# Seven block products in the down projection, weight sums made in DRAM, value columns copied by ScalarE

## The chip, the cores and the metric

The kernel runs on one core of a Trainium2 chip. The metric is the device time of one execution in microseconds, the median of the runs shown. Times within an execution come from the hardware profiler and are counted from the first instruction.

## What is computed

One layer of a hybrid encoder block on 512 tokens of width 1024, after 16 learned meta tokens:

```python
xn = rmsnorm(h, norm_mix_g)
sb_q, sb_k, sb_v, df_q, df_k, df_v = split(xn @ w_in)       # 8 heads of 128 in each of the two branches
o_sb = stick_breaking_attention(sb_q, sb_k, sb_v)           # strictly causal per frame, no softmax
o_df = rmsnorm(differential_attention(df_q, df_k, df_v))    # two softmax maps, block-causal chunks of 64
gates = sigmoid(xn @ w_gate + b_gate)
merged = gates[0] * (o_sb @ w_br_sb) + gates[1] * (o_df @ w_br_df)
h = h + merged @ w_out
hn = rmsnorm(h, norm_ffn_g)
a = silu(hn @ w_ffn_gate) * (hn @ w_ffn_up)                 # 512 x 2816
h = h + a @ w_ffn_down                                      # 2816 x 1024: the down projection
y = rmsnorm(h, norm_final_g)                                # the 512 tokens, meta tokens dropped
```

All data is float32. To keep its precision, the kernel cuts each operand of a product into a high part (a copy rounded to the matmul format) and a low part (what the rounding left), and makes three matmuls for each block: high by high, high by low, low by high. This is `split` (L74 to L76) and `mm3` (L224 to L229). The copy is a ScalarE cast, the difference a VectorE subtraction.

## The kernel before

**Weights.** `stream` lists all weights in the order of their use, in chunks of 512 KB: `cols` are 1024 rows by 128 columns, `rows` are 256 rows by 512 columns. `stage_one` (L128 to L145) issues the load of the next chunk from the SP queue into one of three buffers `wst` (`wsu` for some chunks). `generic` then splits it into `wh` and `wl`, of which there are four each. `READY` and `STAGE` say how many chunks ahead this is done.

**Heads.** The eight heads of the stick-breaking branch and then the eight of the differential branch are generators (`sb_head`, `df_head`). At each `yield n` the main loop (L927 to L962) runs n units of other work: projections for the next head (`halves`, `kv_units`, `seven_units`), parts of the branch output projection (`y_units`) and `turn`, which transposes the next head's values. From the third stick-breaking head on, its keys and values come from seven block products (`seven_units`).

`turn` (L464 to L478) transposes the value rows and gathers 16 columns from each 128 of them into `v_s`, by four GpSimd copies, which a fifth transposition then reads:

```python
for t in range(NQ):
    nc.gpsimd.tensor_copy(v_s[:, 32 * t:32 * t + NM], vT[:, (t + 1) * P:(t + 1) * P + NM])
nc.tensor.transpose(p5[:, 0:P], v_s, ident)
```

Other work of GpSimd in the heads: the bias of a differential head, its squares (`sq`, `sql`) for the head's norm, the stores of `y_units` to DRAM (from the third on they accumulate, L733), and transfers that swap the halves of the keys' high and low parts (`dk`, `dqk`, L620).

**SwiGLU.** For each 128 columns of the 2816, gate and up are made together by seven products of half-size blocks (`first`, `second`, `third`, with the weight sums of `c1` to `c4`). The result, transposed, is `aT`: 128 partitions by 22 row blocks by 512 tokens.

**Down projection.** `accumulate` (L1009 to L1048) runs over the two halves of 512 output columns; for each it goes through the 22 row blocks, and for each of these through four tiles of 128 tokens, with three matmuls of 512 columns a tile, into four banks. In the second half the last token tile is cut in two pieces of 256 columns, and the last six row blocks are done tile by tile, so that the tiles end one after the other. A finished bank is added to the residual `hres` by VectorE; then come the sum of squares (ScalarE), the gain (GpSimd), the root, the scaling and the store (`finish`). Weights for it are split by `generic`, activations by `act_parts`, each row block once for each half.

**Order.** The prologue is ordered by hand (`manual_schedule`); from `order.close()` (L923) on, a planner orders each engine's instructions by its own costs and by the order of the program. `tc.high_priority` moves single instructions ahead. Each engine works through its instructions in order.

Of the kernel before, what the change touches and what calls it, by code (L numbers as in the profile page):

```python
# [16 lines left out]
P = 128  # L17
# [23 lines left out]
def block_kernel(ctx: ExitStack, tc: tile.TileContext, x, meta, norm_mix_g, w_in, w_gate, b_gate,  # L41
# [31 lines left out]

    def split(hi, lo, src, lo_eng=None, hi_copy=None):  # L74
        (hi_copy or nc.scalar.copy)(hi, src)  # L75
        (lo_eng or nc.vector).tensor_tensor(lo, src, hi.bitcast(F32), op=ALU.subtract)  # L76
# [43 lines left out]
    first_ffn = at_of["fg", 1]  # L120
    staged, loaded = [], {}
# [6 lines left out]
    def stage_one():  # L128
        n = len(staged)
        if n == len(stream):  # L130
            return False
        key, view, c0, cw, k0, k1 = stream[n]

        if key[0] == "fu" and key[1]:
            if "w" not in fpools:
                return False
            st = fpools["w"].tile([P, KT, P], F32, tag="wsu", bufs=2, name="wsu")
        elif sevens(key) and key[2] == 1:
            st = fpools["a"].tile([P, KT, P], F32, tag="wsu", name="wsu")
        else:  # L140
            st = wpool.tile([P, k1 - k0, cw], F32, tag="wst", bufs=3, name="wst")
# [317 lines left out]
    def v_units(key, d):  # L459
        vT = d["vT"] = ap_.tile([P, L], F32, tag="vT", bufs=1, name="vT")  # L460

        def turn():
# [11 lines left out]
            for t in range(NQ):  # L474
                nc.gpsimd.tensor_copy(v_s[:, 32 * t:32 * t + NM], vT[:, (t + 1) * P:(t + 1) * P + NM])  # L475
# [450 lines left out]
    todo = []  # L926
    for br in range(2):  # L927
# [4 lines left out]
        for h in range(NH):  # L932
# [76 lines left out]
    def accumulate(pool, name, act, nk, half, tail, done, banks, pieces=None):  # L1009
# [6 lines left out]
        extra = z_tile()[:, 0] if pieces else None  # L1016

        def step(k, t, c0, c1):
# [3 lines left out]
            mm3((acc[t] if c0 == 0 else extra)[:, c0:c1],  # L1022
                [(ah[:, q], al[:, q], wh[:, k % 2, c0:c1], wl[:, k % 2, c0:c1])], k == 0, k == nk - 1)


        def cuts(t):
            return ((0, 256), (256, 512)) if t == NQ - 1 and pieces else ((0, 512),)

        for k in range(nk - tail):
            for t in range(NQ):  # L1030
                for c0, c1 in cuts(t):
                    step(k, t, c0, c1)
        for t in range(NQ):
            for c0, c1 in cuts(t):
                for k in range(nk - tail, nk):
                    step(k, t, c0, c1)
                cs = slice(half * 512 + c0, half * 512 + c1)
                nc.vector.tensor_tensor(hres[:, t, cs], hres[:, t, cs], (acc[t] if c0 == 0 else extra)[:, c0:c1], op=ALU.add)  # L1038
                sq = pool.tile([P, 512], F32, tag="y_sb", bufs=2, name="sq")
                s0, s1 = ssq[t][:, 0:1], ssq[t][:, 1:2]  # L1040
                nc.scalar.activation(sq[:, c0:c1], hres[:, t, cs], AF.Square, accum_out=(s1 if half else s0))
                if half == 0:
                    nc.vector.tensor_scalar(s0, s0, 1.0 / D, EPS, op0=ALU.mult, op1=ALU.add)
                elif c1 < 512:
                    nc.vector.scalar_tensor_tensor(s0, s1, 1.0 / D, s0, op0=ALU.mult, op1=ALU.add)
                if pieces:
                    pieces(t, cs)
# [90 lines left out]
    with tc.tile_pool(name="ffn", bufs=1) as fp:  # L1138
# [10 lines left out]
        jobs += [(generic, n) for n in range(at_of["down", 0, 0], len(stream))]  # L1149
# [61 lines left out]
        dw, acts = None, []  # L1211

        def act_parts(upto):

            for i in range(len(acts), min(2 * NFF, upto)):
                pool, tag, bufs = ((dw, "da", 4), (fw, ("wsu", "s21")[i % 2], 2))[i % 8 < 4]
                a = pool.tile([P, 2, SEQ], F32R, tag=tag, bufs=bufs, name="da")
                split(a[:, 0], a[:, 1], aT[:, i % NFF])
                acts.append(a)

        def act(half, k):
            act_parts(half * NFF + k + 3)
            return acts[half * NFF + k][:, 0], acts[half * NFF + k][:, 1]
# [22 lines left out]
        fpools["down"] = down_weights  # L1246
        ov = out[0].rearrange("(t p) d -> p t d", p=P)
# [50 lines left out]
```

## Time and profile before

| | us |
|---|---|
| median of 3 runs (lowest, highest) | 985.83 (984.46, 989.97) |
| the profiled execution, its span | 988.4, 986.6 |
| busy: TensorE, VectorE, ScalarE, GpSimd | 964.2, 670.7, 574.2, 170.1 |
| first and last matmul of the down projection | 854.82, 978.60 |

The span runs from the first to the last instruction; the execution's own time is 1.8 us longer. The profile names the tile that an instruction writes and those that it reads (`wl<-wst,wh`), its line (a helper's line stands for all that call it: L75 and L76 are the casts and subtractions of `split`, L227 to L229 the three matmuls of `mm3`), and, in brackets, how long the engine stood idle before it and what released it. PE is TensorE, DVE VectorE, ACT ScalarE, POOL GpSimd, SP the queue of plain transfers. Busy times of engines overlap; a wait costs something only where it lies on the way to the end.

### The profile page before, as it was taken

The numbers are of one execution on the slowest core, as the hardware profiler recorded it, in microseconds if no ns is written. First come the engines' busy times: TensorE is split into PE (matmuls) and PEld (weight loads), VectorE is DVE, ScalarE is ACT, GpSimd is POOL, SyncE is SP. The second block draws the span as 40 slices with busy tenths as digits, with TensorE's granted clock in tenths as the row PEclk, the third lists the DMA queues.
The fourth block names the chain that finished last, engine by engine and source line by source line (L and its number), as shares of the span: only waits on it lengthen the run. The fifth ranks groups of instructions, "written<-read, shape, count | busy, mean of one in ns | idle before, by whom it ended". The sixth has DMA issues, their size and how long they took to land.

```text
span 986.6 us, 16202 instructions
## 1 busy us (share of the span) xinstructions
PE 964.2 (98%) x6216; PEld 869.1 (88%) x6217; DVE 670.7 (68%) x1243; ACT 574.2 (58%) x1094; POOL 170.1 (17%) x214
## 2 busy tenths in 40 slices
PE   8899999999999999999999999989999999999996
PEld 6798888898899998899878888879999999988885
DVE  7798687766566876667724434798888888754644
ACT  7566666666566666666763433675555555743533
POOL 3300111111243322343225320000000000000103
PEclk9999999999999999999999999999999999999999
DMA  7312434455665533656659623232424333333212
GB/s 217 86 43 65 129 102 112 97 124 128 129 134 126 133 113 121 130 118 140 129 144 280 194 89 104 64 108 86 128 86 120 95 109 106 110 105 107 86 44 86
DMA packets 140240, 114.12 MB, mean 116 GB/s; under 512 B 4961, under 2 KB 115714, under 8 KB 140162
## 3 DMA queue, kind: packets, MB, share of 16 engines
q1 hardware_dynamic: 129810, 89.29, 30.0%
q0 software_dynamic: 10192, 23.73, 12.8%
q8 instruction: 49, 0.80, 0.3%
q14 instruction: 29, 0.24, 0.1%
q10 hardware_dynamic: 160, 0.07, 0.0%
HBM read 89.87 MB, written 18.87 MB: 110 GB/s over the span
## 4 chain that ended last, share of the span: by engine, by line
PE 90%; ACT 4%; DVE 4%; POOL 1%; issue 1%; DMA 0%; DVEq 0%; ACTq 0%; SPq 0%; POOLq 0%
PE mm L227 21%; PE mm L229 21%; PE mm L228 21%; PE z L227 6%; PE z L229 6%; PE z L228 6%; PE z L638 1%; PE z L637 1%; POOL v_s L475 1%; PE tr L493 1%; PE z L493 1%; PE tr L469 1%; ACT wh L75 1%; PE z L521 1%; DVE wl L76 0%
## 5 line engine op out<-in xcount | busy, mean ns | idle before, releaser
L76 DVE TENSOR_TENSOR wl<-wst,wh 128x1024 fp32r<-128x1024 f32 (+1 forms) x150 | 169.6, 1134 | 110.3 <-ACT wh L75 110.3
L75 ACT CAST wh<-wst 128x1024 fp32r<-128x1024 f32 (+1 forms) x150 | 146.2, 975 | 126.3 <-PE mm L228 70.0
L227 PE MATMUL mm<-xT_h,wh 128*128 128x264 f32 (+2 forms) x656 | 214.6, 327 | 0.5 <-ACT xT_h L830 0.5
L228 PE MATMUL mm<-xT_l,wh 128*128 128x264 f32 (+2 forms) x656 | 213.4, 325 | 0.5
L229 PE MATMUL mm<-xT_h,wl 128*128 128x264 f32 (+2 forms) x656 | 212.7, 324 | 0.0
L228 PEld LDWEIGHTS mm<-xT_l,wh 128*128 128x128 f32 x656 | 123.6, 188 | 10.3 <-DVE xT_l L831 1.3
L227 PEld LDWEIGHTS mm<-xT_h,wh 128*128 128x128 f32 x656 | 123.8, 189 | 10.0 <-ACT xT_h L830 0.9
L229 PEld LDWEIGHTS mm<-xT_h,wl 128*128 128x128 f32 x656 | 123.6, 188 | 10.0
L228 PE MATMUL mm<-hT_l,wh 128*128 128x256 f32 x284 | 80.5, 284 | 0.7 <-DVE hT_l L1081 0.7
L227 PE MATMUL mm<-hT_h,wh 128*128 128x256 f32 x284 | 80.1, 284 | 0.5 <-DVE sg L1176 0.5
L229 PE MATMUL mm<-hT_h,wl 128*128 128x256 f32 x284 | 80.1, 283 | 0.0
L475 POOL COPY v_s<-vT 128x16 f32<-128x16 f32 x64 | 31.9, 528 | 157.8 <-DVE vT L405 79.1
L228 PEld LDWEIGHTS mm<-hT_l,wh 128*128 128x128 f32 x284 | 53.7, 189 | 1.1 <-DVE hT_l L1081 1.1
L641 DVE CUSTOM_DVE_ANT_0 pr<-z,bias 128x144 f32<-128x144 f32 (+3 forms) x64 | 31.0, 502 | 34.9 <-PE z L638 34.7
L227 PEld LDWEIGHTS mm<-hT_h,wh 128*128 128x128 f32 x284 | 53.4, 189 | 0.9 <-DVE sg L1176 0.8
L229 PEld LDWEIGHTS mm<-hT_h,wl 128*128 128x128 f32 x284 | 53.6, 189 | 0.0
L227 PE MATMUL mm<-o_h,wh 128*128 128x512 f32 x128 | 53.1, 415 | 0.0
L229 PE MATMUL mm<-o_h,wl 128*128 128x512 f32 x128 | 50.8, 397 | 0.0
L228 PE MATMUL mm<-o_l,wh 128*128 128x512 f32 x128 | 50.1, 392 | 0.3 <-DVE o_l L709 0.3
L1262 POOL TENSOR_TENSOR outs<-hres,gF 128x512 f32<-128x512 f32 x4 | 5.1, 1291 | 262.3 <-DVE hres L1038 261.3
L227 PE MATMUL mm<-t_h,wh 128*128 128x256 f32 x168 | 47.5, 283 | 1.3 <-ACT wh L75 1.0
L228 PE MATMUL mm<-t_l,wh 128*128 128x256 f32 x168 | 47.3, 281 | 1.1 <-DVE t_l L1096 1.1
(330 smaller groups left out, 2534.3 us busy)
## 6 DMA issues: line engine op xcount, KB each, us to landing
wst<-in_w_in_dram SPq DMA_DIRECT2D x40, 512.0 KB, 4.2
wst<-in_w_ffn_gate_dram SPq DMA_DIRECT2D x22, 512.0 KB, 3.8
wst<-in_w_ffn_down_dram SPq DMA_DIRECT2D x22, 512.0 KB, 3.5
wsu<-in_w_ffn_up_dram SPq DMA_DIRECT2D x21, 512.0 KB, 3.8
y_df<-y_out POOLq DMA_DIRECT2D x32, 256.0 KB, 5.2
wst<-in_w_gate_dram SPq DMA_DIRECT2D x16, 512.0 KB, 5.5
wst<-in_w_br_sb_dram SPq DMA_DIRECT2D x8, 512.0 KB, 4.1
wst<-in_w_br_df_dram SPq DMA_DIRECT2D x8, 512.0 KB, 4.0
```

Of the source, the lines that this page charges most:

```text
L75: (hi_copy or nc.scalar.copy)(hi, src)
L76: (lo_eng or nc.vector).tensor_tensor(lo, src, hi.bitcast(F32), op=ALU.subtract)
L227: nc.tensor.matmul(ps, lhsT=ah, rhs=bh, start=(start and i == 0), stop=False, skip_group_check=skip)
L228: nc.tensor.matmul(ps, lhsT=ah, rhs=bl, start=False, stop=False, skip_group_check=skip)
L229: nc.tensor.matmul(ps, lhsT=al, rhs=bh, start=False, stop=(stop and i == n - 1), skip_group_check=skip)
L469: nc.tensor.transpose(pt[:, j * P:(j + 1) * P], vT[:, j * P:(j + 1) * P], ident)
L475: nc.gpsimd.tensor_copy(v_s[:, 32 * t:32 * t + NM], vT[:, (t + 1) * P:(t + 1) * P + NM])
L493: nc.tensor.transpose(pt[:, (t - j) * P:(t - j + 1) * P], blocks(t, j * P, (j + 1) * P), ident)
L521: nc.tensor.matmul(ps.rearrange("p (t q) -> p t q", q=P)[:, :, lo_rows:P], lhsT=vf[:, 1], rhs=a_s[:, 0:4 * qn], start=False, stop=True)
L637: nc.tensor.matmul(o, lhsT=q[c][:, qs], rhs=k[c][:, 0, k0:k1], start=True, stop=False)
L638: nc.tensor.matmul(o, lhsT=q[c][:, qs], rhs=k[c][:, 1, k0:k1], start=False, stop=True)
L641: nc.vector.tensor_tensor_reduce(po, zz, bb, scale=1.0, scalar=-3.0e38, op0=ALU.add, op1=ALU.max, accum_out=mx[:, t, c:c + 1])
```

## The change

The down projection is seen as a 2 x 2 product: the row blocks in two halves of 11, the output columns in two halves of 512, the tokens in two halves of 256. It is made by seven products of half-size blocks instead of eight, each 11 row blocks by 512 columns by 256 tokens. Three of the seven use raw blocks of the weights (a11, a12, a22), four use sums of blocks (s1 to s4); four use sums of blocks of the activations (t1 to t4), which VectorE makes during the stage.

The weight sums are made in DRAM during the heads, by 48 transfers on GpSimd's queue: 24 that copy a block, then 24 that accumulate onto it (`sum_job`). One is issued after every second unit of the heads, and each waits for the last ScalarE cast of `split` that stands before it in the program. The sums are then staged like other weights. In the stage, four more buffers for staged weights (`slots`) lie where the low parts of the SwiGLU's input were, and the block t2 where its high parts were.

In `turn`, one ScalarE copy of 64 columns takes the place of the four GpSimd copies.

```diff
     def split(hi, lo, src, lo_eng=None, hi_copy=None):
-        (hi_copy or nc.scalar.copy)(hi, src)
+        cast["last"] = (hi_copy or nc.scalar.copy)(hi, src)
...
-    for half in range(2):
-        for k0 in range(0, NFF, 2):
-            rows(("down", half, k0), w_fd, half * 512, k0)
+    NK = NFF // 2
+    DK = range(0, NK, 2)
+    w_sum = {(n, k0): sums_dram.tile([P, 2, 512], F32, name=f"d{n}_{k0}") for n in ("s1", "s2", "s3", "s4") for k0 in DK}
+    raw_at = {"a11": (0, 0), "a12": (NK, 0), "a21": (0, 512), "a22": (NK, 512)}
+    DOWN = (("a11", "b11", 0), ("a12", "b21", 1), ("s1", "t1", 2), ("s2", "t2", 0), ("s4", "b22", 2), ("s3", "t3", 0),
+            ("a22", "t4", 0))
...
+    def sum_job(to, of, k0, add):
+        src = raw_down(of, k0) if of in raw_at else w_sum[of, k0][:, 0:min(2, NK - k0)]
+        dst = w_sum[to, k0][:, 0:min(2, NK - k0)]
+        kw = dict(accum_op=ALU.add, max_dma_last_dim=2048) if add else {}
+        paced = mybir.DependencyInfo(mybir.DependencyClass.Sync, mybir.DependencyReason.DATA)
+        tc.add_manual_dep(nc.gpsimd.dma_start(dst, src, **kw).ins, cast["last"].ins.name, paced)
+
+    background = [(to, of, k0, i > 3) for i, (to, of) in enumerate(
+        (("s1", "a21"), ("s2", "a11"), ("s3", "a21"), ("s4", "a12"), ("s1", "a22"), ("s3", "a11"), ("s2", "s1"), ("s4", "s2")))
+        for k0 in DK]
...
+        if n >= first_down + 3 and "slots" not in fpools:
+            return False
...
+            slot = (n - first_down) % 7 - 3 if n >= first_down else -1
+            if slot < 0:
+                st = wpool.tile([P, 1024 // cw, cw], F32, tag="wst", bufs=3, name="wst")[:, 0:k1 - k0]
+            else:
+                st = fpools["slots"][:, slot, 0:k1 - k0]
...
-            for t in range(NQ):
-                nc.gpsimd.tensor_copy(v_s[:, 32 * t:32 * t + NM], vT[:, (t + 1) * P:(t + 1) * P + NM])
+            nc.scalar.copy(v_s.rearrange("p (t q) -> p t q", q=32)[:, :, 0:NM],
+                           vT[:, NM:L].rearrange("p (t q) -> p t q", q=P)[:, :, P - NM:P])
...
                 for _ in range(min(n, len(units))):
                     units.pop(0)()
+                    unit_count[0] += 1
+                    if background and unit_count[0] % 2 == 0:
+                        sum_job(*background.pop(0))
...
-                split(a[:, 0], a[:, 1], aT[:, i % NFF])
+                src, sign = block(b, k0), -1.0 if b == "t2" else 1.0
+                nc.scalar.activation(a[:, 0, 0:n], src, AF.Copy, scale=sign)
+                nc.vector.scalar_tensor_tensor(a[:, 1, 0:n], src, sign, a[:, 0, 0:n].bitcast(F32), op0=ALU.mult, op1=ALU.subtract)
...
+        def token_sum(name, k0):
+            b11, b12, b21, b22 = block("t1", k0), block("t3", k0), block("b21", k0), block("b22", k0)
+            to, x, y, op = {"t1": (b11, b11, b12, ALU.subtract), "t2": (block("t2", k0), b11, b22, ALU.add),
+                            "t3": (b12, b22, b12, ALU.subtract), "t4": (b21, block("t2", k0), b21, ALU.subtract)}[name]
+            nc.vector.tensor_tensor(to, x, y, op=op)
...
-            stage(at_of[key] + STAGE)
+            stage(at_of[key] + READY + 6)
...
-        accumulate(dw, "down", act, NFF, 0, 0, lambda t: None, "z")
-        accumulate(dw, "down", act, NFF, 1, 6, finish, "mm", gained)
+        for ph, (w, b, e) in enumerate(DOWN):
+            i0 = ph * len(DK)
+            steps = [(i0 + k // 2, k % 2) for k in range(NK)]
+            tail = 6 if ph == 6 else 3
+            first_k = (lambda k: k == 0) if fresh[e] == ph else (lambda k: False)
+            for k in range(0, NK - tail, 2):
+                i = i0 + k // 2
+                while todo and len(todo) > 24 - i / 1.55:
+                    token_sum(*todo.pop(0))
+                for t in range(2):
+                    for j in range(min(2, NK - tail - k)):
+                        if ph == 6 and t:
+                            step(i, j, t, 0, 256)
+                            step(i, j, t, 256, 512, start=k + j == 0)
+                        else:
+                            step(i, j, t, start=first_k(k + j))
+            for t in range(2):
+                for c0, c1 in ((0, 256), (256, 512)) if ph == 6 and t else ((0, 512),):
...
+                    if w == "a12":
+                        to_res(t, D1, acc[0][t], add)
+                        to_res(t, D1, ps, add)
+                        summed(t, D1)
+                    elif w == "s1":
+                        to_res(2 + t, D2, ps, sub)
+                    elif w == "s2":
+                        to_res(2 + t, D1, ps, add)
+                    elif w == "s4":
+                        to_res(2 + t, D1, ps, add)
+                        summed(2 + t, D1)
+                    elif w == "s3":
+                        with tc.high_priority(offset=EVAC):
+                            to_res(2 + t, D2, ps, sub)
+                            if t:
+                                to_res(t, slice(768, D), ps[:, 256:512], sub)
+                        summed(2 + t, D2)
+                        gained(2 + t, D2)
+                        finish(2 + t)
+                    elif w == "a22":
+                        to_res(t, cs, ps[:, c0:c1], sub)
+                        summed(t, cs)
+                        gained(t, cs)
+                        if c1 == 512:
+                            finish(t)
```

`DOWN` names for each product the weights, the activations and the accumulator; the accumulator 0 is used by four products and read at three of their ends. `to_res` adds a bank to or subtracts it from the residual, `step` is three matmuls, `act_parts` makes the activations' parts three chunks ahead.

More of the change, by code (lines that the diff above doesn't have):

```diff
@@ L1007, in block_kernel, with accumulate @@
     ssq = [small.tile([P, 2], F32, tag=f"ssq{t}", bufs=2, name="ssq") for t in range(NQ)]
-    def accumulate(pool, name, act, nk, half, tail, done, banks, pieces=None):
+    def accumulate(pool, name, act, nk, half, tail, done, banks):
         if banks == "z":
@@ L1021, in step @@
             q = slice(t * P, (t + 1) * P)
[L1022 to L1027, printed above, removed]
+            mm3(acc[t], [(ah[:, q], al[:, q], wh[:, k % 2], wl[:, k % 2])], k == 0, k == nk - 1)
+        cs = slice(half * 512, (half + 1) * 512)
         for k in range(nk - tail):
             for t in range(NQ):
[L1031 to L1032 removed]
+                step(k, t)
         for t in range(NQ):
[L1034 to L1047, printed above, removed]
+            for k in range(nk - tail, nk):
+                step(k, t)
+            nc.vector.tensor_tensor(hres[:, t, cs], hres[:, t, cs], acc[t], op=ALU.add)
+            sq = pool.tile([P, 512], F32, tag="y_sb", bufs=2, name="sq")
+            s0, s1 = ssq[t][:, 0:1], ssq[t][:, 1:2]
+            nc.scalar.activation(sq, hres[:, t, cs], AF.Square, accum_out=(s1 if half else s0))
+            if half == 0:
+                nc.vector.tensor_scalar(s0, s0, 1.0 / D, EPS, op0=ALU.mult, op1=ALU.add)
             done(t)
@@ L1148, in block_kernel @@
             jobs += [(c2, f), (c3, f)] + [(c1, f + 1)] * (f + 1 < NFF) + [(c4, f)]
-        jobs += [(generic, n) for n in range(at_of["down", 0, 0], len(stream))]
+        jobs += [(generic, n) for n in range(first_down, len(stream))]
         made = {"n": 0}
@@ L1255, in finish, with to_res, summed @@
             nc.sync.dma_start(ov[:, t, 512:D], o[:, 512:D])
-        outs = []
+        outs = {}
+        ssq = [small.tile([P, 2], F32, tag=f"ssq{t}", bufs=2, name="ssq") for t in range(NQ)]
+        D1, D2 = slice(0, 512), slice(512, D)
+        def to_res(t, cs, ps, op):
+            nc.vector.tensor_tensor(hres[:, t, cs], hres[:, t, cs], ps, op=op)
+        def summed(t, cs):
+            sq = dw.tile([P, 512], F32, tag="y_sb", bufs=2, name="sq")[:, 0:cs.stop - cs.start]
+            s0, s1 = ssq[t][:, 0:1], ssq[t][:, 1:2]
+            nc.scalar.activation(sq, hres[:, t, cs], AF.Square, accum_out=(s1 if cs.start else s0))
+            if cs.start == 0:
+                nc.vector.tensor_scalar(s0, s0, 1.0 / D, EPS, op0=ALU.mult, op1=ALU.add)
+            elif cs.stop < D:
+                nc.vector.scalar_tensor_tensor(s0, s1, 1.0 / D, s0, op0=ALU.mult, op1=ALU.add)
@@ L1266, in block_kernel, with step @@
-        accumulate(dw, "down", act, NFF, 0, 0, lambda t: None, "z")
-        accumulate(dw, "down", act, NFF, 1, 6, finish, "mm", gained)
+        zt = [z_tile() for _ in range(2)]
+        acc = [[zt[0][:, 0], zt[0][:, 1]], [mm_tile(), mm_tile()], [zt[1][:, 0], zt[1][:, 1]]]
+        extra = mm_tile()
+        add, sub = ALU.add, ALU.subtract
+        todo = [(n, k0) for n in ("t1", "t2", "t3", "t4") for k0 in DK]
+        def step(i, j, t, c0=0, c1=512, start=False, stop=False):
+            w, b, e, k0 = order_of[i]
+            act_parts(i + 3)
+            wh, wl = weights(("down", w, k0))
+            a, q = acts[i], slice(t * P, (t + 1) * P)
+            ps = extra if c0 else acc[e][t]
+            mm3(ps[:, c0:c1], [(a[:, 0, j, q], a[:, 1, j, q], wh[:, j, c0:c1], wl[:, j, c0:c1])], start, stop, True)
```

58 lines of the change are left out of this document (44 added, 14 removed).

## The prediction

> **What bounds the kernel now.** I read the page first: parts 1 and 4.
>
> ```profile
> span 986.6 us, 16202 instructions
> ...
> PE 964.2 (98%) x6216; PEld 869.1 (88%) x6217; DVE 670.7 (68%) x1243; ACT 574.2 (58%) x1094; POOL 170.1 (17%) x214
> ...
> PE 90%; ACT 4%; DVE 4%; POOL 1%; issue 1%; DMA 0%; DVEq 0%; ACTq 0%; SPq 0%; POOLq 0%
> ```
>
> TensorE is busy nearly throughout and is 90% of the chain that ended last, so a matmul left out should be worth its whole pace, if no other engine steps in. The share is an average, so next I took the windows: a stretch and its length, the busy time (and instructions) of PE, PEld, DVE, ACT and POOL in it, the granted clock, the share of the DMA engines and GB/s.
>
> ```profile
> 650.00:700.00 50.00, 47.55 (x395) 46.94 (x394) 44.89 (x68) 30.11 (x47) 0.59 (x1) 1.00 0.40 117
> ...
> 750.00:800.00 50.00, 50.00 (x421) 50.00 (x420) 42.07 (x66) 27.53 (x45) 0.00 (x0) 1.00 0.37 106
> ...
> 917.00:978.70 61.70, 61.70 (x334) 53.45 (x332) 29.80 (x50) 25.64 (x48) 8.65 (x7) 1.00 0.18 65
> ```
>
> The last row is the down projection's second half: TensorE never idle, VectorE half free. The 750 row (SwiGLU) shows VectorE at 84% with TensorE still never idle; the 650 row has VectorE at 90% and TensorE short by 2.45 us. These two say how far VectorE can be loaded. The timeline gives the matmuls' pace in the down projection.
>
> ```profile
> 854.82 0.40 PE L227 MATMUL z<-wh,da 128*128 128x512 f32 x1
> ...
> 855.53 0.30 PE L227 MATMUL mm<-t_h,wh 128*128 128x256 f32 x1
> ...
> 858.40 0.40 PE L227 MATMUL z<-wh,da 128*128 128x512 f32 x1
> ...
> 963.99 0.39 PE L229 MATMUL mm<-wh,da 128*128 128x512 f32 x1
> ...
> 974.18 0.39 PE L229 MATMUL mm<-wh,da 128*128 128x512 f32 x1
> 974.41 0.28 PE L227 MATMUL mm<-wh,da 128*128 128x256 f32 x1
> ...
> 978.60 0.28 PE L229 MATMUL z<-wh,da 128*128 128x256 f32 x1
> ```
>
> 963.99 to 974.18 holds 45 steps of 512 columns: 0.2264 us each, start to start. 974.41 to 978.60 holds 35 steps of 256 columns: 0.1197 us. The stage has 22 rows of blocks x 2 halves x 4 token tiles x 3 products = 528 matmuls, 66 of them cut in two: 462 x 0.2264 + 132 x 0.1197 = 120.4 us. Seen: 854.82 to 978.60 less the 2.87 us of SwiGLU between 855.53 and 858.40, 120.9 us. The pace explains the stage; nothing else is in it.
>
> **Down projection, TensorE.** Seven products of 11 rows x 2 token tiles x 3 = 462 matmuls replace 528; 33 of them are cut in two. 429 x 0.2264 + 66 x 0.1197 = 105.0 us: 15.4 us less. The bank waits are new: the sixth product is evacuated (two or three VectorE additions) while the seventh wants the same banks, with 6 matmuls (1.4 us) between; I take +1.0, with 0 and one full round of two additions, +1.4, as ends. The last token tile is still cut in two and ends in the same steps (978.60 to the span's end, 8.0 us): 0.
>
> **Down projection, VectorE.** More work moves here: 77 half-chunks of weights to split instead of 44, 24 token sums that were not there, 16 additions into the residual instead of 9. Start-to-start prices from the timeline, and two groups of ScalarE:
>
> ```profile
> 858.14 1.23 DVE L76 TENSOR_TENSOR wl<-wst,wh 128x1024 fp32r<-128x1024 f32 x1 [0.54 <-ACT wh L75]
> 859.29 0.42 DVE L1200 TENSOR_TENSOR sg<-z,qx 128x256 f32<-128x256 f32 x1
> 859.62 0.68 DVE L76 TENSOR_TENSOR da<-aT,da 128x512 fp32r<-128x512 f32 x1
> 860.22 1.22 DVE L76 TENSOR_TENSOR wl<-wst,wh 128x1024 fp32r<-128x1024 f32 x1
> ...
> L75 ACT CAST wh<-wst 128x1024 fp32r<-128x1024 f32 x123 | 129.5, 1053 | 119.4 <-PE mm L228 70.0 <-PE z L229 37.8 <-issue 3.9
> ...
> L75 ACT CAST da<-aT 128x512 fp32r<-128x512 f32 x44 | 27.0, 621 | 20.5 <-PE z L229 18.6 <-DVE wl L76 1.9
> ```
>
> So 1.15 us for 1024 elements, 0.33 for 256, 0.60 for 512. The first six products hold all the token sums: weights 30 x 1.15 + 6 x 0.60 = 38.1; activations 30 x 0.60 + 6 x 0.33 = 20.0; token sums 20 x 0.60 + 4 x 0.33 = 13.3; residual additions 12 x 0.60 + 0.33 = 7.5; small ones 1.5. Together 80.4 us, beside 396 x 0.2264 = 89.7 us of TensorE: 90%, between the two rows of the windows and nearer the 650 row. At that row's 90% nothing is lost (0); at 84% the six products would take 80.4 / 0.84 = 95.7, +6.0. I take +2.0, since weights and activations are made three chunks ahead and the seventh product has no sums. ScalarE has 1.05 + 0.62 us per chunk, for a cast and an activation copy, of 12 x 0.2264 = 2.7: free.
>
> The stream of weights doubles its rate: 20.2 MB in 105 us.
>
> ```profile
> q1 hardware_dynamic: 4912, 9.44, 24.0%
> ...
> wst<-in_w_ffn_down_dram SPq DMA_DIRECT2D x16, 512.0 KB, 3.5
> ```
>
> That is the transfers' answer for 860 to 975: 9.44 MB in 24.0% of 115 us, 342 GB/s when active, so 20.2 MB fill 59 of 105 us: 0. The fourth chunk goes to a buffer in the old activations and can start only when SwiGLU's last matmul is done (858.40): landing 3.5, cast and subtraction 1.1 + 1.2, ready at 864.2. Three chunks of 12 matmuls keep TensorE until 858.40 + 33 x 0.2264 = 865.9. Hidden by 1.7 us; gone if it lands that much later.
>
> **Value columns on ScalarE.** Four GpSimd copies per head become one ScalarE copy.
>
> ```profile
> PE tr L476 <- POOL v_s L475: 5.2, 2, 4.2
> 32.54 4.69 POOL L475 COPY v_s<-vT 128x16 f32<-128x16 f32 x1 [8.51 <-ACT vT L480]
> ...
> 37.17 0.48 ACT L471 CAST vh<-tr 128x384 fp32r<-128x384 f32 x1
> ...
> 38.92 2.36 POOL L475 COPY v_s<-vT 128x16 f32<-128x16 f32 x3
> ...
> 41.33 0.47 PE L476 MATMUL tr<-ident,v_s 128*128 128x128 f32 x1 [4.20 <-POOL v_s L475]
> ...
> 41.84 0.27 ACT L477 COPY vf<-tr 128x128 f32<-128x128 f32 x1 [4.20 <-PE tr L476]
> 40.00:42.00 2.00, 0.67 (x3) 0.44 (x4) 1.22 (x2) 0.15 (x1) 1.28 (x3) 0.80 0.12 36
> 42.00:44.00 2.00, 2.00 (x10) 1.89 (x10) 0.00 (x0) 1.77 (x4) 0.00 (x0) 0.50 0.00 0
> 44.00:46.00 2.00, 2.00 (x9) 1.57 (x9) 0.53 (x1) 1.97 (x4) 0.00 (x0) 0.85 0.00 0
> 80.00:90.00 10.00, 8.98 (x67) 7.93 (x66) 8.73 (x16) 6.47 (x14) 1.33 (x3) 1.00 0.37 110
> ```
>
> The first line is of the waits, then timeline, then windows. In head 0 a copy of 16 columns took 4.69 us, three more followed the bias, and TensorE stood 4.20 us for them; ScalarE was idle from 37.65 on. With a ScalarE copy (0.27, the price of its neighbour) the transpose could go at about 38.1: 3.2 us. The granted clock fell to 0.50 after that idle, which cost 0.67 x 0.20 + 2 x 0.50 + 2 x 0.15 = 1.4 us; the second wait (1.0 us, in the 80 to 90 row) left the clock at 1.00, so a gap of 1 us should too. With 0.7 of that second wait: 5.3 us at most. VectorE is busy up to 41.2 there with weights TensorE wants next, so I take -4.3. Ends: -6.6 (both waits and the dip whole) and +4.3 (16 new copies all on the path).
>
> The Trainium skill, "TensorE: Matmul & The Clock Gate" (HAM clock gate), says that an idle window of about 3.4 us halves the clock; by that rule the 4.20 us gap explains the dip and a gap of 1 us pays none, as the rows have it. The Trainium skill, "SBUF — State Buffer" (Who interferes with whom), says that a VectorE instruction with two inputs in SBUF shuts out a GpSimd instruction that reads SBUF; by it the 4.69 us copy waited for VectorE's run of sums, and a copy on ScalarE never would, so the term would be the whole -5.3 and the time 969.6.
>
> **Weight sums in DRAM.** 48 transfers on GpSimd's queue, one after every second unit of the heads, 512 KB each (a sixth of them half): 23.1 MB written, half of it accumulated. After 50 units of the first branch and 8 a head, the last comes in the sixth head of the second branch, so the stages from 460 on have none.
>
> ```profile
> q0 software_dynamic: 4676, 11.28, 27.3%
> q1 hardware_dynamic: 25047, 15.73, 24.3%
> ...
> dk<-dk POOLq DMA_DIRECT2D x8, 264.0 KB, 5.5
> 307.95 0.54 POOL L620 DMA_DIRECT2D dk<-dk  x1 [0.41 <-DVE dk L617]
> ...
> 319.43 0.28 PE L637 MATMUL z<-dk,dq 128*128 128x256 f32 x1
> L76 POOL TENSOR_TENSOR sql<-sq,sqh x7: 1305/1306/1315, 289.3 to 469.5; 128x512 fp32r<-128x512 f32 x7
> 319.31 1.31 POOL L76 TENSOR_TENSOR sql<-sq,sqh 128x512 fp32r<-128x512 f32 x1 [0.73 <-ACT sqh L75]
> ...
> 323.14 0.39 PE L702 MATMUL tr<-sql,ones_r 128*128 128x512 f32 x1
> L733 POOL DMA_DIRECT2D y_df<-y_out x24 | 21.1, 960 | 35.0 <-ACT y_out L729 33.5 <-ACT a_h L495 1.3
> ```
>
> From 240 to 460 us GpSimd's queue moved 11.28 MB in 27.3% of 220 us: 5.3 us per MB, so 2.8 us a job. The squares (sql) come seven times between 289.3 and 469.5, so a head takes 30 us, and four jobs in it add 11 us to DMA engines that are 52% busy: 90%. Weights are staged three chunks ahead (chunks of 7.5 us), so a landing twice as long stays hidden. Queued behind a job on GpSimd: the swap of key halves (dk), issued at 307.95 and wanted at 319.43, landing 5.5, so 6.0 us to spare; two jobs ahead of it take 5.6. The squares for the head's norm end at 320.62 and are wanted at 323.14, 2.5 us to spare; an issue costs GpSimd 0.96, and a job waits there for a ScalarE cast, which holds the squares behind it. I take +1.5 over the heads; ends 0 and six heads x 1.7 = +10.
>
> **Sum.** -15.4 + 1.0 + 2.0 - 4.3 + 1.5 = -15.2. The profiled execution took 988.4 around its span of 986.6, so 973.2 for one like it; the median of the runs is 985.83, 2.6 below, and 15.2 off it gives 970.6.
>
> **Rivals.**
> *VectorE becomes the bound of the down projection.* For it: 90% by the sum, and it waits for casts in between. Against it: the 650 row. At 84% the term is +6.0 for +2.0: 974.6; with a bubble at each of six product ends of one weight split (1.15), 981.
> *The copies on ScalarE gain nothing*, because TensorE meets the next late thing in head 0, VectorE's weights and sums that end at 41.2. For it: VectorE has no gap from 38 to 41.2. Against it: the matmuls behind the transpose wanted nothing of that. 974.9.
> *The sums choke GpSimd's queue* (slower). If an accumulation that reads and writes DRAM costs double, 10.6 us per MB, a head's four jobs take 22 us, its y stores (1.05 MB) and key swaps (0.54 MB) 8.5 more at 5.3: 31 of 30 us, the queue backs up and every dk is late. It decides from 2.5 us of wait in each of six heads (15.2 / 6), three jobs ahead of a dk; at four it is 5.4 x 6 = 32 us: 1003. Against it: y stores that accumulate are in that 5.3 us per MB. The Trainium skill, "SBUF — State Buffer" (the trap in which VectorE blocks DMA), says that VectorE's two-port copies starve GpSimd of descriptors, which would lengthen the issue; by it the sums would choke sooner, but no issue in the rows above is long.
>
> **How the numbers follow.** Forecast 0.58 (its own range 964 to 976); VectorE bound 0.14; copies gain nothing 0.12; queue chokes 0.09; the rest (all terms at their good ends, or a new order of the heads that costs some us) 0.07. Four fifths lie in 962 to 980. A change under 0.5%, 4.9 us, can't be told from none here: faster needs 980.9, so 0.85; same 0.07; slower 0.08.
>
> **What would show it.** The down projection's first to last matmul about 108 us with TensorE near 100%; VectorE near 90% in its first six products; no idle at 37 to 41 us and clock 1.00 there; no waits of L637 or L702 in the second branch. Idle TensorE in the heads, or a stage over 113 us, would make me wrong.

## The result: 971.4 us, and the profile after

The changed kernel takes 971.38 us in the median (970.56 to 972.62), beside 987.9 (984.46 to 989.97) for the kernel before: a ratio of 0.9833, 95% interval 0.981 to 0.9856. The forecast was 970.6. The profiled executions, which the rest of the text compares, have spans of 986.6 and 969.1: 17.5 us less. The runs of the kernel before fall in two groups, 984 to 986 and 988 to 990, and its profiled execution (988.4) is of the upper one, so that the medians differ by 1 us less, 16.5.

The page of the changed kernel, parts 1, 3 and 4:

```profile
span 969.1 us, 16156 instructions
...
PE 948.4 (98%) x6117; PEld 853.8 (88%) x6118; DVE 701.2 (72%) x1292; ACT 588.0 (61%) x1128; POOL 183.8 (19%) x198
...
q0 software_dynamic: 19408, 46.80, 23.8%
...
PE 86%; DVE 6%; ACT 4%; DMA 3%; issue 1%; DVEq 0%; ACTq 0%; SPq 0%
```

TensorE is as full as before (98%) with 15.8 us less to do. DMA, 0% of the chain before, is 3% of it now. Most of this is one load of `wst` that takes 16.52 us from 219.11 on and cost nothing: TensorE is busy for 140.00 of 140.00 us from 100 to 240. The load that did cost is a smaller part of the 3%, `wsu`, below.

The timeline of the changed kernel gives the down projection's borders (L262 to L264 are now the three matmuls of `mm3`, L77 and L78 the cast and the subtraction of `split`):

```profile
852.27 0.40 PE L262 MATMUL z<-wh,da 128*128 128x512 f32 x1
...
852.98 0.30 PE L262 MATMUL mm<-t_h,wh 128*128 128x256 f32 x1
...
856.02 0.40 PE L262 MATMUL z<-wh,da 128*128 128x512 f32 x1
...
947.28 0.28 PE L264 MATMUL mm<-wh,da 128*128 128x256 f32 x1
947.67 0.38 PE L262 MATMUL mm<-wh,da 128*128 128x256 f32 x1
948.35 0.50 PE L262 MATMUL z<-wh,da 128*128 128x512 f32 x1 [0.29 <-DVE hres L1308]
...
962.33 0.28 PE L264 MATMUL mm<-wh,da 128*128 128x256 f32 x1
```

So the 17.5 us come off in three places. Before the stage: its first matmul starts at 852.27 for 854.82, 2.5 us earlier. In the stage: 852.27 to 962.33 less 3.04 of SwiGLU (852.98 to 856.02) is 107.0, for 120.9: 13.9 less. Behind it: 962.33 to 969.1 is 6.8, for 8.0: 1.2 less. (The SwiGLU within the stage takes 0.2 more.)

The same stage in windows, one for each of the first six products and one for the seventh (a stretch and its length, busy time and instructions of PE, PEld, DVE, ACT and POOL, clock, DMA share, GB/s):

```profile
855.50:870.40 14.90, 14.90 (x69) 12.17 (x68) 13.10 (x19) 10.48 (x17) 0.00 (x0) 1.00 0.87 291
870.40:885.30 14.90, 14.90 (x68) 12.33 (x67) 14.90 (x23) 8.41 (x12) 0.00 (x0) 1.00 0.70 217
885.30:900.30 15.00, 15.00 (x67) 12.24 (x66) 14.52 (x23) 9.75 (x16) 0.00 (x0) 1.00 0.62 197
900.30:915.20 14.90, 14.90 (x67) 12.16 (x66) 11.09 (x14) 8.63 (x12) 0.00 (x0) 1.00 0.59 197
915.20:930.20 15.00, 15.00 (x67) 12.22 (x66) 11.09 (x14) 9.08 (x13) 0.40 (x1) 1.00 0.61 190
930.20:945.30 15.10, 15.10 (x72) 12.58 (x71) 12.32 (x16) 9.86 (x17) 3.61 (x3) 1.00 0.38 121
945.30:962.60 17.30, 16.89 (x99) 14.55 (x97) 11.72 (x24) 9.14 (x21) 7.83 (x6) 1.00 0.18 67
```

A product of 66 steps at 0.2264 us is 14.94: the first six run at that pace, though VectorE is busy for the whole of the second. Its sum over the six is 77.0 us of 89.8, near the 80.4 counted. The largest loss lies at the seventh: three gaps from 947.28 to 948.68 take about 0.9 us more than the steps do, and the row at 948.35 names the addition into the residual that frees the bank.

The opening of the heads in the changed kernel, first the timeline, then windows:

```profile
36.68 0.23 ACT L509 COPY v_s<-vT 128x64 f32<-128x64 f32 x1
...
37.03 0.27 PE L511 MATMUL tr<-ident,v_s 128*128 128x128 f32 x1
...
66.63 0.69 DVE L208 TENSOR_TENSOR s<-wsu 128x512 f32<-128x512 f32 x1 [3.30 <-DMA wsu<-in_w_in_dram]
...
87.04 0.69 DVE L208 TENSOR_TENSOR s<-wsu 128x512 f32<-128x512 f32 x1 [2.00 <-DMA wsu<-in_w_in_dram]
```

```profile
40.00:50.00 10.00, 10.00 (x72) 9.41 (x71) 10.00 (x16) 5.31 (x9) 0.00 (x0) 1.00 0.19 53
...
60.00:100.00 40.00, 36.77 (x257) 33.30 (x256) 32.29 (x51) 25.79 (x49) 3.81 (x6) 1.00 0.53 163
```

The transpose of head 0 follows its copy at once (37.03 for 41.33 before), and 40 to 50 has no idle and no dip of the clock. But further on VectorE waits for `wsu`, a staging buffer of which there is one: the load that ends the wait at 66.63 was issued at 60.97, when VectorE had last read the buffer. Between 60 and 100 TensorE is 3.2 us short. The row of before for that stretch has 1.0:

```profile
60.00:100.00 40.00, 38.98 (x287) 35.80 (x285) 33.87 (x55) 27.84 (x52) 3.24 (x8) 1.00 0.23 67
```

### The profile page after: what moved, and what is told of

It reads as the page before. It is cut to its first block, busy times and chain, and to the rows that moved or that the text cites. A ratio compares the mean times of both kernels' runs of the same rounds, so it can differ in the third digit from the quotient of the medians.

```text
span 969.1 us, 16156 instructions
## 1 busy us (share of the span) xinstructions
PE 948.4 (98%) x6117; PEld 853.8 (88%) x6118; DVE 701.2 (72%) x1292; ACT 588.0 (61%) x1128; POOL 183.8 (19%) x198
## 3 DMA queue, kind: packets, MB, share of 16 engines
q0 software_dynamic: 19408, 46.80, 23.8%
## 4 chain that ended last, share of the span: by engine, by line
PE 86%; DVE 6%; ACT 4%; DMA 3%; issue 1%; DVEq 0%; ACTq 0%; SPq 0%
PE mm L264 19%; PE mm L263 19%; PE mm L262 19%; PE z L262 7%; PE z L263 7%; PE z L264 7%; DMA wst<-in_w_in_dram 2%; PE z L673 1%; PE z L672 1%; DVE wl L78 1%; PE tr L528 1%; PE z L528 1%; ACT wh L77 1%; PE tr L504 1%; PE z L556 0%
## 5 line engine op out<-in xcount | busy, mean ns | idle before, releaser
L262 PE MATMUL mm<-xT_h,wh 128*128 128x264 f32 (+2 forms) x656 | 214.3, 327 | 0.5 <-ACT xT_h L865 0.5
L78 DVE TENSOR_TENSOR wl<-wst,wh 128x1024 fp32r<-128x1024 f32 (+1 forms) x146 | 162.3, 1116 | 72.1 <-ACT wh L77 72.0
L264 PE MATMUL mm<-xT_h,wl 128*128 128x264 f32 (+2 forms) x656 | 212.8, 324 | 0.0
L77 ACT CAST wh<-wst 128x1024 fp32r<-128x1024 f32 (+1 forms) x146 | 140.2, 962 | 103.0 <-PE mm L263 70.0
L262 PEld LDWEIGHTS mm<-xT_h,wh 128*128 128x128 f32 x656 | 123.6, 188 | 10.0 <-ACT xT_h L865 0.9
L264 PEld LDWEIGHTS mm<-xT_h,wl 128*128 128x128 f32 x656 | 123.4, 188 | 9.9
L262 PE MATMUL mm<-hT_h,wh 128*128 128x256 f32 x284 | 80.3, 285 | 0.6 <-DVE sg L1202 0.6
L264 PE MATMUL mm<-hT_h,wl 128*128 128x256 f32 x284 | 80.1, 283 | 0.0
L1322 POOL TENSOR_TENSOR outs<-hres,gF 128x512 f32<-128x512 f32 x4 | 7.2, 1799 | 283.2 <-DVE hres L1308 278.1
L141 POOL DMA_DIRECT2D ds<-in_w_ffn_down_dram x36 | 28.5, 791 | 156.0 <-ACT wh L77 106.0
L262 PEld LDWEIGHTS mm<-hT_h,wh 128*128 128x128 f32 x284 | 53.4, 189 | 1.0 <-DVE sg L1202 0.8
L264 PEld LDWEIGHTS mm<-hT_h,wl 128*128 128x128 f32 x284 | 53.6, 189 | 0.0
L262 PE MATMUL mm<-o_h,wh 128*128 128x512 f32 x128 | 53.1, 415 | 0.0
L262 PE MATMUL z<-wh,da 128*128 128x512 f32 (+1 forms) x132 | 50.9, 386 | 0.3 <-DVE hres L1308 0.3
L264 PE MATMUL mm<-o_h,wl 128*128 128x512 f32 x128 | 50.8, 397 | 0.0
L263 PE MATMUL z<-wl,da 128*128 128x512 f32 (+1 forms) x132 | 50.4, 382 | 0.0
```

What stands on the lines that cost most here:

```text
L77: cast["last"] = (hi_copy or nc.scalar.copy)(hi, src)
L141: tc.add_manual_dep(nc.gpsimd.dma_start(dst, src, **kw).ins, cast["last"].ins.name, paced)
L262: nc.tensor.matmul(ps, lhsT=ah, rhs=bh, start=(start and i == 0), stop=False, skip_group_check=skip)
L263: nc.tensor.matmul(ps, lhsT=ah, rhs=bl, start=False, stop=False, skip_group_check=skip)
L264: nc.tensor.matmul(ps, lhsT=al, rhs=bh, start=False, stop=(stop and i == n - 1), skip_group_check=skip)
L1322: nc.gpsimd.tensor_tensor(outs[t][:, D1], hres[:, t, D1], gF[:, D1], op=ALU.mult)
```

## The experiments

**1. The changed kernel with the four GpSimd copies back.**

```diff
-            nc.scalar.copy(v_s..., vT...)
+            for t in range(NQ):
+                nc.gpsimd.tensor_copy(v_s[:, 32 * t:32 * t + NM], vT[:, (t + 1) * P:(t + 1) * P + NM])
```

> The changed kernel with the four GpSimd copies of the value columns back. The changed kernel's trace starts the down projection 2.5 us earlier than before, with TensorE's stop of 4.2 us at 37 us gone, the clock at 1.00 there, and 4.0 us of other waits new between 50 and 90 us. Theory: the copies are worth these 2.5 us, so 2.5 us slower than the changed kernel, span about 971.6, the stop at 37 to 41 us back and the waits after it gone. Rival: with 24 transfers in GpSimd's queue in the first branch, the copies wait behind them too: 6 us or more slower. Second rival: the copies were never worth anything beyond a new order, within 1 us.

Measured: 975.62 (973.23 to 978.34), 0.9869 of before [0.9847, 0.9891], some 4 us above the changed kernel, for 2.5 in the theory. A line of its waits (total, times, longest), then windows:

```profile
PE tr L511 <- POOL v_s L510: 4.1, 2, 3.1
```

```profile
40.00:50.00 10.00, 9.01 (x31) 7.29 (x32) 5.03 (x8) 3.36 (x6) 0.94 (x2) 0.66 0.19 54
...
80.00:90.00 10.00, 7.49 (x50) 6.53 (x49) 10.00 (x16) 7.25 (x14) 2.54 (x5) 0.89 0.48 148
```

The stop for `v_s` is back, and the clock is granted 0.66 behind it, and 0.89 behind another idle at 80 to 90 that the changed kernel also has, without a dip. So the copies gain, and the rival that they were worth less than 1 us is refuted; the 6 us or more of the other rival, in which they wait behind the transfers too, is not reached by the median. How much they gain alone, the next run shows.

**2. The kernel before with only the ScalarE copy.** The edit of experiment 1 the other way round, on the kernel before.

> The kernel before with only the ScalarE copy of the value columns. If the waits that are new between 50 and 90 us are VectorE's own work coming due (theory), they come here too: 2 to 3 us faster than before. If they come from the transfers of the weight sums that delay the staged weights (rival), they don't come here, and the whole stop, its clock dip and the second wait are won: 6 to 6.6 us faster.

Measured: 983.5 (982.43 to 983.65), 0.9946 [0.9928, 0.9964]. The down projection's first matmul starts at 848.89, 5.9 us earlier than before and 3.4 earlier than in the changed kernel. By the medians (989.15 for the kernel before, run beside it) the gain is 5.65, near the rival's 6 and not the theory's 2 to 3. Windows:

```profile
40.00:50.00 10.00, 10.00 (x74) 9.52 (x73) 10.00 (x16) 5.08 (x9) 0.00 (x0) 1.00 0.00 0
...
60.00:100.00 40.00, 38.96 (x272) 35.40 (x271) 33.13 (x52) 27.07 (x51) 0.00 (x0) 1.00 0.29 83
```

The rest of the change delays the stage by 3.4 us, and 2.2 of these (38.96 against 36.77) lie between 60 and 100.

**3. No sums in DRAM: raw blocks staged in their place.** The four products that need sums take raw blocks, so the result is not the layer's; only the time is read.

```diff
-    raw_at = {"a11": (0, 0), "a12": (NK, 0), "a21": (0, 512), "a22": (NK, 512)}
+    raw_at = {"a11": (0, 0), "a12": (NK, 0), "a21": (0, 512), "a22": (NK, 512),
+              "s1": (NK, 512), "s2": (0, 0), "s3": (NK, 0), "s4": (0, 512)}
...
-    background = [(to, of, k0, i > 3) for ...]
+    background = []
```

> The changed kernel without the 48 transfers that make weight sums; the four products that used sums read raw blocks of the same sizes instead, so only the transfers are gone. Theory: they cost TensorE nothing, as no wait in the second branch names them although the DMA engines are 93 to 98% busy there: within 1 us of the changed kernel. Rival (the prediction's term): 1.5 us faster. Rival of the delayed weights: 4 us faster, without the waits between 50 and 90 us.

Measured: 968.82 (968.03 to 969.14), 0.9798 [0.9778, 0.9818]. The stage starts at 849.53, 2.7 us earlier than with the sums:

```profile
60.00:100.00 40.00, 38.88 (x270) 35.10 (x269) 32.95 (x51) 26.74 (x51) 0.00 (x0) 1.00 0.28 81
```

So it is the transfers that cost the 2 to 3 us, and they cost them here, in the first branch. VectorE's waits for `wsu` between 50 and 110 are 3.1 us in this run and 5.3 in the changed kernel, and TensorE is 2.1 us less short between 60 and 100. The theory that the transfers cost nothing is wrong; the rival of delayed weights is right on the place, with 2.6 us (medians) of its 4.

**4. No token sums: VectorE freed in the stage.** The four products that need token sums take raw blocks, so here too only the time is read.

```diff
-                return part["t2"][:, k0:k0 + n]
+                return aT[:, k0:k0 + n, T1]
...
-        todo = [(n, k0) for n in ("t1", "t2", "t3", "t4") for k0 in DK]
+        todo = []
```

> The changed kernel without the 24 token sums in the down projection; the products read raw blocks of activations instead. VectorE loses 13.3 us of 80.4 in the first six products. Theory: VectorE was near full (14.9 of 14.9 us in one product) and still not the bound: within 0.7 us of the changed kernel, the first six products 89.8 us as they are. Rival (the prediction's term): 2 us faster.

Measured: 970.19 (969.97 to 972.41), 0.9818 [0.9797, 0.9839]; span 968.5, 0.6 below the changed kernel's. From its first to its last matmul the stage takes 109.58 (852.12 to 961.70), for 110.06 in the changed kernel.

```profile
870.40:885.30 14.90, 14.90 (x67) 12.33 (x67) 11.78 (x17) 9.14 (x15) 0.00 (x0) 1.00 0.61 203
```

The product in which VectorE was busy for 14.90 of 14.90 us now has it at 11.78, and takes as long. A full VectorE cost nothing in this product, and at most 0.5 us in the whole stage.

**5. Every token sum made twice: VectorE loaded 13.7 us more.**

```diff
+            nc.vector.tensor_tensor(spare[0][:, 0:min(2, NK - k0)], b12 if name != "t3" else b21, b22, op=op)
             nc.vector.tensor_tensor(to, x, y, op=op)
...
+        spare.append(t2f[:, NM + NK * 256:NM + (NK + 2) * 256].rearrange("p (k t) -> p k t", t=256))
```

The second addition goes into columns that nothing reads.

> The changed kernel with a second VectorE addition of the same size beside each of the 24 token sums, into columns that nothing reads: 13.3 us more of VectorE in the first six products. Without the token sums the down projection was as long as with them, so VectorE was not its bound; VectorE was busy 77.0 of 89.9 us in the first six products. Theory: 77 + 13 = 90 us, VectorE becomes the bound at the products with the most sums, 2 to 5 us slower than the changed kernel, and all of it in the down projection. Rival: weights and activations made three chunks ahead hide this too, within 1 us.

Measured: 974.31 (974.06 to 976.47), 0.9862 [0.9843, 0.988]. Windows of the fifth to the seventh product, and two of the waits:

```profile
915.20:930.20 15.00, 15.00 (x67) 12.30 (x66) 14.97 (x23) 8.84 (x13) 0.15 (x1) 1.00 0.57 193
930.20:945.30 15.10, 14.64 (x68) 12.06 (x67) 15.10 (x22) 9.49 (x15) 3.72 (x2) 1.00 0.36 122
945.30:962.60 17.30, 14.76 (x77) 12.38 (x78) 13.38 (x25) 8.10 (x17) 6.38 (x5) 1.00 0.17 62
```

```profile
PE mm L263 <- DVE wl L78: 1.7, 1, 1.7
PE z L262 <- DVE rs L353: 1.1, 1, 1.1
```

Here VectorE is busy for 89.1 of the first six products' 89.8 us (14.21, 14.90, 15.00 and 14.90 in the four that are not shown); TensorE keeps its pace for five of them and falls 3.0 us short at the end (0.46 + 2.54; in the changed kernel 0.41). The stage takes 112.39 (853.00 to 965.39), 2.3 more than in the changed kernel, of the 2.9 between the medians: within the theory's 2 to 5. So the margin is real but small. That late work is paid from the stock of parts made ahead, and shows only when the stock is used up, fits the late start of the loss but was not tried by itself.

**6. The transfers without the pacing wait.**

```diff
-        tc.add_manual_dep(nc.gpsimd.dma_start(dst, src, **kw).ins, cast["last"].ins.name, paced)
+        nc.gpsimd.dma_start(dst, src, **kw)
```

> The changed kernel without the wait of each of the 48 transfers for the last ScalarE cast; everything else as it is. Theory: the pace matters, since GpSimd's queue has nothing else to hold the first 24 copies (12 MB, 50 us of all DMA engines at 4.5 us per MB), which then crowd the staged weights of the prologue: 10 us slower or more, TensorE idle in the first 100 us. Rival: the planner keeps the program's order anyway, and GpSimd's other work spaces them: within 2 us.

Measured: 1011.67 (1011.14 to 1012.45), 1.0235 [1.0214, 1.0256]: 40 us slower than with the wait. Windows, then waits between 30 and 100 (total, times, longest):

```profile
30.00:60.00 30.00, 21.06 (x116) 18.14 (x115) 18.05 (x28) 12.98 (x22) 13.86 (x18) 0.77 0.90 283
60.00:100.00 40.00, 31.13 (x231) 28.97 (x230) 24.43 (x39) 18.93 (x36) 12.15 (x13) 0.92 1.12 209
100.00:240.00 140.00, 125.44 (x799) 111.86 (x799) 95.40 (x155) 83.90 (x162) 14.78 (x20) 0.93 0.54 125
```

```profile
DVE s L208 <- DMA wsu<-in_w_in_dram: 14.8, 1, 14.8
ACT wh L77 <- DMA wst<-in_w_in_dram: 11.3, 2, 8.0
```

The transfers run as early as GpSimd reaches them (the last is issued at 111.90, at 392.82 in the changed kernel) and fill the DMA engines where the first heads stage their weights, for which VectorE then waits up to 14.8 us. TensorE is idle for 32.4 of these 210 us, for 4.0 in the changed kernel, and its clock is granted at 0.77, 0.92 and 0.93, for 1.00 there. It is the kind of cost that experiment 3 took away, about fifteen times as large.

**7. All transfers in the second branch, eight a head.** Nothing is issued in the first 50 units; then two at every second unit.

```diff
-                    if background and unit_count[0] % 2 == 0:
+                    for _ in range(2 if background and unit_count[0] > 50 and unit_count[0] % 2 == 0 else 0):
                         sum_job(*background.pop(0))
```

> The changed kernel with all 48 transfers in the first six heads of the second branch, two after every second unit, eight a head instead of four. The first branch has none. Theory: with 8 x 0.52 MB a head at 4.5 us per MB the DMA engines, 52% busy before, are asked for 115%, GpSimd's queue backs up, the key swaps land later than the 11.5 us they have, and TensorE waits for them (score matmuls of dk): the prediction's rival made to happen, 15 us slower than the changed kernel or more. Rival: the backlog only moves the sums later, and the first branch gets its 3 us back: 3 us faster.

Measured: 971.63 (970.18 to 973.16), 0.983 [0.981, 0.985], no different from the changed kernel: neither side's number. Windows, the only long wait of TensorE from 240 to 460, and a row of the timeline ahead of it:

```profile
300.00:360.00 60.00, 60.00 (x397) 54.92 (x397) 41.57 (x110) 38.02 (x92) 31.71 (x34) 1.00 1.03 226
360.00:420.00 60.00, 56.90 (x371) 51.60 (x369) 39.65 (x104) 39.36 (x93) 25.58 (x29) 1.00 1.09 240
```

```profile
PE tr L528 <- DVE pr L706: 3.1, 1, 3.1
```

```profile
362.52 1.05 ACT L77 CAST wh<-wst 128x1024 fp32r<-128x1024 f32 x1 [5.08 <-DMA wst<-in_w_in_dram]
```

The 2 us of the first branch came back (38.88 of 40 at 60 to 100) and 3.1 went in the second, once, when the DMA engines had been full for over 60 us. It too is a late weight: ScalarE stood 5.08 us for a chunk in `wst`, and next in its order behind that cast came an activation (L700, at 363.88) whose result VectorE's `pr` needs, for which TensorE waited until 367.68. So at eight transfers a head even a load with three buffers came late. The waits for `dk` that the choke rival rests on did not come even at eight transfers a head.

**8. Start after unit 18, at the same pace.** The first transfer is issued at 102.88 us, behind both waits for `wsu`.

```diff
-                    if background and unit_count[0] % 2 == 0:
+                    if background and unit_count[0] > 18 and (unit_count[0] % 2 == 0 or unit_count[0] > 100):
```

> The changed kernel with the 48 transfers started after unit 18 (three heads) at the same pace, so the last comes in the last head. Copies alone started the down projection 5.9 us before the kernel before did, the changed kernel 2.5 us, and its VectorE waited 3.3 and 2.0 us at 66 and 87 us for the staged values' weights (wsu), which has one buffer. Theory: these waits are all that the sums cost, so they go: the down projection starts at about 849 us, 3 us faster than the changed kernel, some 968. Rival: the sums cost the same wherever they are, since the DMA engines are fuller in the second branch: no gain.

Measured: 970.78 (969.32 to 971.64), 0.9818 [0.9797, 0.984]: under the changed kernel's median by 0.6, less than the runs scatter. Windows:

```profile
60.00:100.00 40.00, 38.93 (x271) 35.18 (x270) 33.55 (x51) 26.88 (x50) 0.00 (x0) 1.00 0.27 80
420.00:460.00 40.00, 39.51 (x263) 35.54 (x262) 27.15 (x65) 25.71 (x62) 14.98 (x17) 1.00 0.88 198
```

TensorE has its 2.2 us back at 60 to 100 and loses a part where the transfers now end, in the last heads (40.00 of 40.00 in the changed kernel). Weight subtractions (`wl<-wst,wh`) are 2.1 us ahead of the changed kernel's up to 422 us, 1.0 ahead from 439 on, and 0.4 behind from 659 on, where this profiled execution has a dip of the clock (last section). The forecast gain was there but was not kept whole.

**9 and 10. Start after unit 18, two of every three units; and the changed kernel on the same chip.**

```diff
-                    if background and unit_count[0] % 2 == 0:
+                    if background and unit_count[0] > 18 and unit_count[0] % 3 < 2:
```

> The 48 sum jobs start after unit 18 and go in two of every three units, so that they are over at about unit 90, as in the changed kernel; nothing else changes. Theory (the sums cost some 2 us in the first branch's opening heads, because the single-buffered value weights land late there, and 1 us in the last heads when they end late): both are gone, the first product of the down projection starts at about 850, the span is about 967, the time about 968.5, 0.980 to 0.981 of before. Rival (the DMA engines are what is short wherever the sums lie): the denser transfers delay the weights of the later heads, TensorE loses 2 us or more between 150 and 350 in some 20 us stretches, and the time is that of the changed kernel, 971, or above.

> The changed kernel itself, on the same chip as the version with a later and denser schedule, so that the two can be compared directly. Theory: 0.983 to 0.984 of before, and about 2 us above the later and denser one. Rival: the two are equal within 0.5 us.

Measured: 969.68 (968.28 to 970.4; 0.9815 [0.9792, 0.9839]) for the later and denser schedule, 971.83 (970.61 to 973.51; 0.9842 [0.9818, 0.9867]) for the changed kernel. The intervals against the kernel before overlap, but no run of the one is above any run of the other, on one chip: about 2 us, as the theory said, though its 968.5 for the later and denser schedule was 1.2 too low. Windows of the first:

```profile
60.00:100.00 40.00, 38.88 (x269) 35.09 (x269) 32.91 (x51) 26.71 (x51) 0.00 (x0) 1.00 0.28 81
...
280.00:340.00 60.00, 60.00 (x397) 54.92 (x396) 42.16 (x111) 39.62 (x95) 26.77 (x29) 1.00 1.07 215
...
420.00:460.00 40.00, 40.00 (x272) 36.64 (x272) 27.69 (x67) 26.85 (x67) 11.82 (x14) 1.00 0.58 132
```

Both losses are gone, though the DMA engines show a share of 1.07 for 60 us. The rival, that denser transfers delay the later heads by 2 us, fails. It is the fastest of the runs that make the sums. Its span (968.3) is only 0.8 below the changed kernel's 969.1, because this profiled execution had a dip of the clock at 650 to 655 that the other had not (last section): the subtraction that is 2.2 us ahead of the changed kernel's at 652 is followed by one 0.8 ahead at 659.

## Why the prediction was right, point by point

The total, 15.2 us off for 17.5 measured between the profiled executions (16.5 between the medians), came out because errors lay on both sides: the stage gained 1.5 more than forecast, the copies 1.6 and the tail 1.2, while the sums cost up to 1.9 more. That they cancel in part is luck. So is some of the closeness of 970.6 to 971.4: the forecast took its 15.2 off a median of 985.83, and off the 987.9 of the result it would have been 972.7.

*TensorE's share of the down projection: right.* 429 steps of 512 and 66 of 256 columns were counted and are there; 105.0 us counted, 107.0 seen.

*Bank wait at the seventh product: right*, place and size: +1.0 against about 0.9 (the three gaps from 947.28).

*VectorE's fullness: the load right, its price too high.* 80.4 us was counted and 77.0 found, but the +2.0 was taken between two rows of SwiGLU, in one of which TensorE was 2.45 us short beside a VectorE at 90%. Of these, 1.99 lie in the first 5 of its 50 us, where TensorE waits once for VectorE (1.13) and once for ScalarE (0.97); that row was no measure of a load held throughout (windows of before):

```profile
650.00:655.00 5.00, 3.01 (x24) 2.61 (x22) 5.00 (x6) 4.97 (x7) 0.00 (x0) 1.00 0.02 6
```

Experiment 4 puts the price at 0.5 or less; in experiment 5, at 89.1 of 89.8 us, it is 2.3. The rival of a bound VectorE needed some 12 us more work in those six products. About 1 us of the stage's loss beyond the bank wait is spread over many steps, and no wait names it.

*The fourth chunk: right.* No wait of TensorE in the stage names weights; the bank is the only one.

*Value copies: the step that was too small*, -4.3 for -5.9 (experiment 2, by the start of the stage). The transpose went 4.3 us earlier and not 3.2, since ScalarE made the copy (36.68) ahead of the cast `vh` that the prediction put before it. The deduction for VectorE's late weights was not needed: VectorE is busy for 10.00 of 10.00 us at 40 to 50, and TensorE as well. The -5.9 passes even the "5.3 at most" of that step, within its ends. The rival of copies that gain nothing is refuted by the ratio, 0.9946 [0.9928, 0.9964].

*Sums in DRAM: the step that failed in its mechanism.* +1.5 was taken for GpSimd's queue in the second branch: issues, squares and `dk`. There no wait for them came, even at eight transfers a head (experiment 7). The cost is 2.7 us by experiment 3, and 3.4 by experiment 2, which counts all that the rest of the change does ahead of the stage. Some 2 us of it lie in the first heads, where the transfers share the DMA engines with the value weights that VectorE sums out of a single buffer. The prediction had said that a landing twice as long stays hidden. In the changed kernel that holds for `wst`, where even a landing of 16.52 us stayed hidden, but not for `wsu`. A second buffer for `wsu` was not tried. The trace of before had the sign, which was not read: a row of its timeline in which VectorE waits for `wsu`, with the DMA engines at a share of only 0.19 (windows of before, 60 to 80).

```profile
70.09 0.69 DVE L173 TENSOR_TENSOR s<-wsu 128x512 f32<-128x512 f32 x1 [1.43 <-DMA wsu<-in_w_in_dram]
```

The choke rival's price, double for transfers within DRAM, was not met: GpSimd's queue moved its 46.80 MB in 23.8% of 969.1 us, 4.9 us per MB, under the 5.3 of the prediction's row.

*Tail: 0 forecast, 1.2 us gained.* The timelines of the last scalings, before and then after:

```profile
977.74 1.60 DVE L1252 TENSOR_SCALAR outs<-outs,rs 128x512 f32<-128x512 f32 x1
...
977.77 1.29 POOL L1262 TENSOR_TENSOR outs<-hres,gF 128x512 f32<-128x512 f32 x1 [0.92 <-DMA out_dram<-outs]
```

```profile
959.01 1.30 POOL L1323 TENSOR_TENSOR outs<-hres,gF 128x512 f32<-128x512 f32 x1 [1.00 <-DVE hres L1308]
...
960.98 0.48 DVE L1298 TENSOR_SCALAR outs<-outs,rs 128x512 f32<-128x512 f32 x1
```

Before, VectorE's scaling ran beside GpSimd's product and took 1.60 us; after, GpSimd is done at 960.31 and the same scaling takes 0.48. VectorE adds the last bank to the residual only behind it: at 979.86 before, 1.26 us after the start of the last matmul (978.60), and at 962.64 after, 0.31 after it (962.33). So 0.95 of the 1.2 us are this. The Trainium skill, "SBUF — State Buffer" (Who interferes with whom), says that a VectorE instruction in a two-port mode and GpSimd shut each other out for a whole instruction, and that scalings by a scalar can run in such a mode; the two durations agree with it. That the overlap went was luck of the new order, not a part of the change.

Together: -5.9 for the copies, +3.4 for the sums and whatever else the change does ahead of the stage, -13.9 for the stage, -1.2 for the tail and +0.2 for the SwiGLU within the stage make -17.4, of 17.5.

## What to carry to other kernels

A product by seven blocks is worth nearly its full share of matmuls (13.9 of 15.4 us here) where a stage is nothing but matmuls. A second engine whose results are made a few chunks ahead may be nearly full for a while: VectorE was busy for 74.0 of 74.7 us in experiment 5 before TensorE lost anything. As far as these runs go, background transfers cost first where a load has the fewest buffers, here at a DMA share of 0.53, while a load with three buffers cost TensorE time only at eight transfers a head (experiment 7) or, it seems, without the pacing (experiment 6). So look for the single-buffered loads first and start the transfers behind them, at a pace that ends before the last heads. A pace by a wait on the foreground's own work is worth far more (40 us here) than where exactly the transfers are put (2 us).

## What the runs showed of the hardware that was not expected

The DMA engines can be at a share of 1.03 to 1.09 for over 100 us (experiment 7) and of 1.07 for 60 (experiment 9) with 3.1 us lost in the first case and nothing in the second, while at a share of 0.53 (60 to 100, changed kernel) 2.2 us went: the share did not tell the cost.

Idle time of TensorE did not always cost clock: in the changed kernel 80 to 90 has 7.81 of 10 us busy at 1.00, in experiment 1 7.49 at 0.89, and in experiment 4, whose heads are those of the changed kernel, 9.00 at 0.83. In experiment 9's profiled execution there is such a dip at a place that the change did not touch (windows of experiment 9, then of the changed kernel):

```profile
650.00:655.00 5.00, 4.34 (x22) 4.13 (x23) 3.42 (x6) 2.18 (x5) 0.59 (x1) 0.66 0.71 232
```

```profile
650.00:655.00 5.00, 3.75 (x27) 3.35 (x27) 4.92 (x6) 4.04 (x6) 0.59 (x1) 1.00 0.38 113
```

The longest idle of TensorE from 640 to this dip was 1.12 us, so the prediction's reading that a gap of 1 us costs no clock does not hold everywhere. What decides it was not tried. The profiled executions of experiments 7 and 8 have the dip as well (0.83 over 650 to 660); it hides about 1.4 us of the gain in those of experiments 8 and 9.
